# Gate stage of a PEER block: more first product in the steps with row products, upper halves at a step's begin, the high digit's one-hots for 32 tokens

## The chip, the cores and the metric

The kernel runs on one core of a Trainium2 chip. The metric is device microseconds of one execution. The kernel before took 1411.17 us (median of three runs, 1410.4 to 1411.97). Engine names are those of the profile: PE is the matrix engine (PEld its weight loads), DVE the vector engine, ACT the scalar engine, POOL the GpSimd engine, SP the engine that issues most loads.

## The reference

For 512 tokens of width 1024: a normalised input goes through a gating group and an attention group, their joined output is added to the input, and a PEER layer follows, with 16384 experts:

```python
q = (xb @ w_query)                               # 8 heads, 2 halves
sc = einsum('thpd,hpkd->thpk', q, sub_keys)      # 128 keys a half
s_top, i_top = top_k(sc, 16)                     # 16 x 16 candidates
best, pos = top_k(cand, 16)                      # 16 experts a head
g = softmax(best)
h = gelu(einsum('thkd,td->thk', expert_u[eidx], xb))
out = einsum('thk,thkd->td', g * h, expert_v[eidx])
```

So each token uses 128 of the 16384 experts, each with its own gate `g`.

## The kernel before

Of the 512 tokens, 128 gather their experts' rows at the end. The other 384 (three tiles of 128) are computed densely, and 64 of these are mixed: their expert inputs are gathered rows, too. The experts stand as 128 rows of 128. Per row b of experts:

- the **first product** of 320 tokens with the 128 experts of b is a matrix product over 8 slices of the width; each is split in an upper and a lower half, so that a slice costs three matmuls (`mm3`, lines 196 to 198, 128x320). One b is a "tile" of first product: 8 slices, 24 matmuls, then a Gelu on ACT (line 724).
- the tile's weights come by a 512 KB load (`raw`, line 155, SP's queue, three buffers); ACT makes the upper half (`hi`, line 157) and DVE or POOL the lower half (`lo`, line 158: raw minus hi). `hi` and `lo` have five buffers each.
- in the last and longest stage (from 600 us on) the gated activations are multiplied with the rows of V (line 1215), together with the first products that are left.

The **gate stage** lies ahead of that. It turns the 128 chosen experts of each of the 384 tokens into a dense table of gates in DRAM. It runs in 48 steps of 8 tokens (`TC`), and a block of matmuls follows two steps later (`LEAD`). Block m is the product of step m's tokens. A step n does:

- POOL: `bm` (line 981), the second one-hot with the gate in it, from two digit tables `hb` (high digit times gate, 8 wide) and `lb` (low digit, 16 wide).
- PE: block n-2, eight f32 matmuls `pa<-bm,am` (line 998; each stands as two in the profile).
- ACT: two copies `gst<-pa` (line 1001) of that block; after every second step it issues a 1024 KB store of `gst` (line 1005, three buffers).
- DVE: `am` (line 989), the first one-hot; three buffers of `am` and of `bm`.
- in steps 1 to 33 also a gathered row of U for the mixed tokens (POOL issues the gather, line 660) and its **row product** on DVE (`rowe`, line 670).
- every second step, the digits for the next 16 tokens on DVE (lines 970 and 973: `hb`, `hb` times gate, `lb`).
- `some` slices of first product on PE, and at the step's end sometimes one new tile: its load, its `hi` on ACT, its `lo` on DVE or (each fourth) on POOL.

Where a token tile ends, its gates are transposed on PE (lines 959 and 960). At step 33 the row products are through, and `dots` and `weights_early` fold them into the gates.

Order: PE, DVE, ACT and POOL take their instructions of this stage exactly as the code writes them (`manual_schedule`); each queue runs in order, and a waiting instruction holds all behind it. SP's loads are in the order of their issue and wait for a free `raw` buffer. The numbers of the table are `AHEAD` 25, `LAST` 2 and `HELD` 2; `steps` is 48, `own` is 40.

Of the kernel before, what the change touches and what calls it, by code (L numbers as in the profile page):

```python
# [8 lines left out]
F32 = mybir.dt.float32  # L9
F32R = mybir.dt.float32r  # L10
# [3 lines left out]
AF = mybir.ActivationFunctionType  # L14
ALU = mybir.AluOpType
# [4 lines left out]
P = 128  # L20
# [3 lines left out]
KT = D // P  # L24
# [27 lines left out]
BC = 2  # L52
# [3 lines left out]
RAW = 3  # L56
HI = 5
LO = 5
# [5 lines left out]
LEAD = 2  # L64
BH = 8
BL = NB // BH
QT = 16
AHEAD = 25
LAST = 2
HELD = 2  # L70
EASY = 8
SOME = 15
FILL = (0, 1, 2, 3, 4, 4, 3, 3)
# [21 lines left out]
def hybrid_block(tc, x, ln1, w_in, gng, wsT, bsb, qkg, bias, w_out, ln2, wq, skT, uT, ud, vd, out):  # L95
    nc = tc.nc
    ctx = ExitStack()
    with ctx:
# [13 lines left out]
        def big(tag, dt, bufs):  # L112
            return wst.tile([P, 1024], dt, name=tag, tag=tag, bufs=bufs)
# [10 lines left out]
        loads, splits, ready = [], [], []  # L124
# [24 lines left out]
        def load_split(src, eng=nc.vector, **dims):  # L149

            raw = big("raw", F32, RAW)
            hi = big("hi", F32R, HI)
            lo = big("lo", F32R, LO)
            fold = (lambda v: v.rearrange("p (a b) -> p a b", **dims)) if dims else (lambda v: v)
            load = nc.sync.dma_start(fold(raw), src)
            loads[:] = [getattr(load, "ins", load)]
            top = nc.scalar.activation(hi, raw, AF.Copy)  # L157
            ins = eng.tensor_tensor(lo, raw, hi.bitcast(F32), op=ALU.subtract)  # L158
            halved[:] = [getattr(i, "ins", i) for i in (top, ins)]
            if eng is nc.gpsimd:  # L160
                splits[:] = [getattr(ins, "ins", ins)]
            return fold(hi), fold(lo)

        def split_tile(i, eng):

            ready.append((*divmod(i, BC), load_split(uT[i], eng, b=P)))
# [257 lines left out]
        with tc.tile_pool(name="preb", bufs=1, reuse_waits="tile") as preb:  # L424
# [135 lines left out]
            steps = [(t, (h, h + 1)) for t in range(TT) for h in range(0, HB, 2)]  # L560
# [158 lines left out]
        def multiply_tile(whole=False):  # L719
            multiply_some(KT, whole)  # L720
# [215 lines left out]
        def split_next(eng=nc.gpsimd):  # L936
            nonlocal split
            if split < AHEAD * BC:
                split_tile(split, eng)
                split += 1  # L940

        for _ in range(HELD):
            split_next()
# [9 lines left out]
        gp = gp_ctx.enter_context(tc.tile_pool(name="gp", bufs=1, reuse_waits="tile"))  # L953

        def gates_of(t, ff):

            ps = pa()
            for i in range(3):
                nc.tensor.transpose(ps[:, i * P:(i + 1) * P], ff[:, i, :], ident)
            nc.tensor.transpose(ps[:, 3 * P:4 * P], gate[:, t, :], ident)  # L960
            return ps.rearrange("p (a t) -> p a t", a=4)

        def digits(g, q):

            ts_ = slice(q * QT, (q + 1) * QT)
            hb = gp.tile([P, QT, BH], F32, name="hb", tag="hb", bufs=2)
            lb = gp.tile([P, QT, BL], F32, name="lb", tag="lb", bufs=2)
            for i, (d, n) in enumerate(((hb, BH), (lb, BL))):
                full = [P, QT, n]
                nc.vector.tensor_tensor(d, iota_k[:, None, 0:n].to_broadcast(full),  # L970
                                        g[:, 1 + i, ts_, None].to_broadcast(full), op=ALU.is_equal)
                if i == 0:
                    nc.vector.tensor_tensor(d, d, g[:, 3, ts_, None].to_broadcast(full), op=ALU.mult)
            return hb, lb

        def second_one_hot(d, c):

            ts_ = slice(c * TC % QT, c * TC % QT + TC)
            full = [P, TC, BH, BL]
            bm = gp.tile([P, TC, P], F32, name="bm", tag="bm", bufs=LEAD + 1)  # L980
            nc.gpsimd.tensor_tensor(bm.rearrange("p t (h l) -> p t h l", l=BL),  # L981
                                    d[0][:, ts_, :, None].to_broadcast(full),
                                    d[1][:, ts_, None, :].to_broadcast(full), op=ALU.mult)
            return bm
# [9 lines left out]
        def products(am, bm, c, st):  # L994
            for q in range(TC // 4):
                ps = pa()
                for i in range(4):
                    nc.tensor.matmul(ps[:, i * P:(i + 1) * P], am[:, 4 * q + i, :], bm[:, 4 * q + i, :],  # L998
                                     start=True, stop=True)
                t0 = (c * TC + 4 * q) % TG  # L1000
                nc.scalar.copy(st[:, :, t0:t0 + 4], ps.rearrange("p (t b) -> p b t", b=NB))

        def store(n, st):
            gd, (n0, n1) = next((g, r) for g, r in zip(gds, GROUPS) if n < r[1])
            nc.scalar.dma_start(gd[:, :, n - n0, :].rearrange("q p f -> p q f"),
                                st.rearrange("p (q b) t -> p q (b t)", b=GB))
# [15 lines left out]
        steps = NDT // TC  # L1022
# [5 lines left out]
        own = steps - UX // TC  # L1028
        with tc.manual_schedule(engines=engines):
            multiply_tile()  # L1030
            gs[0] = gates_of(GT, ff.pop(0))
            dgs = {0: digits(gs[0], 0)}
            split_next()
            multiply_tile()
            for n in range(steps + LEAD):
                t, c = divmod(n, per)
                if n < steps:
                    bms[n] = second_one_hot(dgs[n * TC // QT], c)
                if n >= LEAD:
                    m = n - LEAD  # L1040
                    if m * TC % TG == 0:
                        st = gp.tile([P, NB, TG], F32, name="gst", tag="gst", bufs=3)
                    products(ams.pop(m), bms.pop(m), m % per, st)
                    if (m + 1) * TC % TG == 0:
                        store(m * TC // TG, st)
                while begun:
                    activate_tile()
                if n < steps:
                    ams[n] = first_one_hot(gs[t], c)
                if n in (1, 2):  # L1050
                    indices_early(NH - 3 + n)
                    ready_early(NH - 3 + n)
                if n:
                    dots_early(LAGE, 1)
                if EASY - 3 < n < own - 7 and n % 8 != 1:
                    gather_early(1, gat, ROWA)
                if t + 1 < ND:
                    if c == per - 5:
                        ff[t + 1] = indices_of(GT + t + 1)
                    if c == per - 3:  # L1060
                        gs[t + 1] = gates_of(GT + t + 1, ff[t + 1])
                if n == own - 7:
                    assert not early
                    dots_early(0)
                    weights_early(0)
                if n == own - 6:
                    weights_early(1)
                if n == own - 4:
                    weights_early(2)
                if n == own - 3:  # L1070

                    late = gates_of(GT + t, ff.pop(t))
                if n == own - 1:
                    gs[t] = late

                    gat_ctx.close()
                    gcp = [ctx.enter_context(tc.tile_pool(name="gcp", bufs=1, side="right", reuse_waits="tile"))]
                if n == steps - 2:
                    load_gates(0, nc.gpsimd, range(1))
                if (n + 2) * TC % QT == 0 and n + 2 < steps:  # L1080
                    t1, c1 = divmod(n + 2, per)
                    dgs[(n + 2) * TC // QT] = digits(late if n + 2 >= own else gs[t1], c1 * TC // QT)

                made = len(ready) * KT + (KT - open_tile[4] if open_tile else 0)
                left = (AHEAD - LAST) * BC * KT - split * KT + made
                some = -(-left // (steps + LEAD - n))
                multiply_some(some)
                if n > 1 and split < (AHEAD - LAST) * BC + HELD and len(ready) < HELD and (n > EASY or n % 2 == 0):
                    split_next(nc.vector if split % 4 else nc.gpsimd)
            while ready or open_tile:  # L1090
                if split == AHEAD * BC and not weights:
                    weights[0] = rows_of_v(0)
                multiply_tile()
                split_next(nc.vector)
                if len(begun) > 1:
                    activate_tile()
            while begun:
                activate_tile()
# [202 lines left out]
```

## Time and profile before

| what | value |
|---|---|
| median of three runs | 1411.17 us |
| profiled execution, own time | 1410.74 us |
| its span | 1409.0 us |
| around the span | 1.7 us |
| gate stage, blocks 0 to 10 | 438.6 to 473.4 us |
| blocks 11 to 33 (with row products) | 473.4 to 545.9 us |
| blocks 34 to 47 (without) | 545.9 to 584.5 us |
| last stage | from 600 us to the end |

All times of the trace are microseconds from the span's start. A window row gives, for each engine, its busy time and in brackets the instructions in that window, then PE's granted clock, the share of the DMA engines' time, and GB/s. In the chain of waits a row is: start, length, what. In a timeline row the bracket at the end is the idle time of that engine ahead of the instruction, and what ended it. Where a timeline merges rows, "x2" is their number. Groups of instructions give busy time and mean ns of one, then the idle time ahead of them. A busy PE is not a PE at its peak, since the ends of matmuls are modelled; so the distance between the starts of blocks says more than busy time.

### The profile page before, as it was taken

How to read it: one execution, taken by the hardware profiler on the slowest of the kernel's cores; microseconds unless marked ns; L12 is line 12 of the kernel's file. 1: busy time of each engine (PE TensorE's matmuls, PEld its weight loads, DVE VectorE, ACT ScalarE, POOL GpSimd, SP SyncE). 2: the span in 40 equal slices, each digit the busy share in tenths (PEclk: the TensorE clock that was granted, in tenths of full speed). 3: DMA queues.
4: the chain of work that ended last, by engine and by line, in shares of the span. 5: the costliest groups of instructions: out<-in, count | busy, mean ns of one | idle time of the engine just before them, and what ended most of it. 6: DMA issues, size and time to landing. Idle time of an engine off the chain costs nothing.

```text
span 1409.0 us, 21692 instructions
## 1 busy us (share of the span) xinstructions
PE 1386.7 (98%) x7838; PEld 1224.6 (87%) x7838; DVE 1154.3 (82%) x2508; ACT 612.0 (43%) x960; POOL 673.0 (48%) x486
## 2 busy tenths in 40 slices
PE   9999999999999989999999999999999999999998
PEld 7887688899899989988898899899889989888887
DVE  5437845898998998678999999898898887889983
ACT  5447635443434445534344444444443333333331
POOL 0002103777778998424555456454464543344520
PEclk9999999999999999999999999999999999999999
DMA  4452316567666999979999999999999998799981
GB/s 165 135 194 76 104 72 199 193 220 271 240 225 222 348 354 281 289 254 355 330 342 348 362 360 342 369 372 359 375 348 383 352 359 337 272 353 363 357 311 60
DMA packets 164330, 396.24 MB, mean 281 GB/s; under 512 B 12880, under 2 KB 75232, under 8 KB 162176
## 3 DMA queue, kind: packets, MB, share of 16 engines
q1 hardware_dynamic: 64640, 194.14, 37.6%
q0 software_dynamic: 48176, 173.46, 33.9%
q10 hardware_dynamic: 51408, 27.27, 6.6%
q8 instruction: 61, 1.00, 0.3%
q14 instruction: 45, 0.37, 0.1%
HBM read 363.34 MB, written 31.46 MB: 280 GB/s over the span
## 4 chain that ended last, share of the span: by engine, by line
PE 78%; DVE 13%; DMA 2%; POOL 2%; issue 2%; ACT 2%; ACTq 0%; DVEq 0%; POOLq 0%
PE pa L1215 23%; PE px L1215 12%; PE pu L196 9%; PE pu L198 9%; PE pu L197 9%; PE pa L998 3%; PE pa L196 3%; PE pa L197 3%; PE pa L198 3%; DVE rowe L670 2%; DVE lo L158 2%; DVE tree L800 1%; DVE am L989 1%; DMA raw<-in_vd 1%; POOL rowe L660 1%
## 5 line engine op out<-in xcount | busy, mean ns | idle before, releaser
L157 ACT ACTIVATE hi<-raw 128x1024 fp32r<-128x1024 f32 x296 | 313.0, 1058 | 448.2 <-DMA raw<-in_uT 120.8
L158 DVE TENSOR_TENSOR lo<-raw,hi 128x1024 fp32r<-128x1024 f32 x244 | 305.7, 1254 | 99.9 <-ACT hi L157 99.1
L1139 POOL DMA_INDIRECT row<-in_ud,eint x128 | 193.0, 1508 | 180.8 <-DVE acc L1152 129.4
L196 PE MATMUL pu<-xch,hi 128*128 128x320 f32 x784 | 247.5, 316 | 3.0 <-ACT act L724 2.8
L1150 POOL DMA_INDIRECT row<-in_vd,eint x128 | 159.7, 1247 | 178.0 <-DVE row L1141 118.6
L198 PE MATMUL pu<-xch,lo 128*128 128x320 f32 x784 | 242.8, 310 | 0.8 <-DVE lo L158 0.8
L197 PE MATMUL pu<-xcl,hi 128*128 128x320 f32 x784 | 242.8, 310 | 0.0
L1215 PE MATMUL pa<-lo,wh 128*128 128x512 f32 x512 | 199.7, 390 | 0.0
L1215 PE MATMUL pa<-hi,wh 128*128 128x512 f32 x512 | 199.4, 389 | 0.0
L158 POOL TENSOR_TENSOR lo<-raw,hi 128x1024 fp32r<-128x1024 f32 x52 | 124.0, 2398 | 119.0 <-ACT hi L157 116.1
L1152 DVE SCALAR_TENSOR_TENSOR acc<-row,hw,acc 128x1024 f32<-128x1024 f32 x128 | 165.2, 1290 | 2.8 <-DMA row<-in_vd,eint 2.5
L1141 DVE SCALAR_TENSOR_TENSOR row<-row,xb 128x1024 f32<-128x1024 f32 x128 | 155.7, 1220 | 10.3 <-DMA row<-in_ud,eint 10.3
L1215 PE MATMUL pa<-hi,wl 128*128 128x512 f32 x512 | 158.5, 389 | 0.0
L196 PEld LDWEIGHTS pu<-xch,hi 128*128 128x128 f32 x784 | 148.0, 189 | 6.1 <-ACT act L724 4.4
L197 PEld LDWEIGHTS pu<-xcl,hi 128*128 128x128 f32 x784 | 148.1, 189 | 1.4
L198 PEld LDWEIGHTS pu<-xch,lo 128*128 128x128 f32 x784 | 147.8, 189 | 1.1 <-DVE lo L158 1.0
L1215 PEld LDWEIGHTS pa<-hi,wh 128*128 128x128 f32 x512 | 96.1, 188 | 20.5
L1215 PEld LDWEIGHTS pa<-hi,wl 128*128 128x128 f32 x512 | 96.1, 188 | 20.3
L1215 PEld LDWEIGHTS pa<-lo,wh 128*128 128x128 f32 x512 | 96.1, 188 | 20.2
L998 PE MATMUL pa<-bm,am 128*128 128x128 f32 x768 | 95.1, 277 | 8.0 <-POOL bm L981 4.2
L998 PEld LDWEIGHTS pa<-bm,am 128*128 128x128 f32 x768 | 90.7, 191 | 11.7 <-POOL bm L981 6.5
L1215 PE MATMUL px<-hi,wh 128*128 128x512 f32 x256 | 100.1, 391 | 0.4 <-ACT hi L157 0.4
(236 smaller groups left out, 2641.6 us busy)
## 6 DMA issues: line engine op xcount, KB each, us to landing
raw<-in_uT SPq DMA_DIRECT2D x128, 512.0 KB
raw<-in_vd SPq DMA_DIRECT2D x128, 512.0 KB
gd<-gst ACTq DMA_DIRECT2D x24, 1024.0 KB
gc<-gd SPq DMA_DIRECT2D x15, 1280.0 KB
raw<-in_w_in SPq DMA_DIRECT2D x19, 512.0 KB
raw<-in_wq SPq DMA_DIRECT2D x16, 512.0 KB
raw<-in_w_out SPq DMA_DIRECT2D x8, 512.0 KB
gc<-gd SPq DMA_DIRECT2D x15, 256.0 KB
```

The costliest lines, as they stand in the source:

```text
L157: top = nc.scalar.activation(hi, raw, AF.Copy)
L158: ins = eng.tensor_tensor(lo, raw, hi.bitcast(F32), op=ALU.subtract)
L196: nc.tensor.matmul(ps, lh[0], rh[0], start=first, stop=False)
L197: nc.tensor.matmul(ps, lh[0], rh[1], start=False, stop=False)
L198: nc.tensor.matmul(ps, lh[1], rh[0], start=False, stop=last)
L670: nc.vector.scalar_tensor_tensor(row, row, 1.0, xbu, op0=ALU.mult, op1=ALU.mult, accum_out=du[:, j:j + 1])
L998: nc.tensor.matmul(ps[:, i * P:(i + 1) * P], am[:, 4 * q + i, :], bm[:, 4 * q + i, :], start=True, stop=True)
L1139: nc.gpsimd.indirect_dma_start(out=row, out_offset=None, in_=ud, in_offset=bass.IndirectOffsetOnAxis(ap=eint[:, j:j + 1], axis=0))
L1141: nc.vector.scalar_tensor_tensor(row, row, 1.0, xb0, op0=ALU.mult, op1=ALU.mult, accum_out=hw[:, j:j + 1])
L1150: nc.gpsimd.indirect_dma_start(out=row, out_offset=None, in_=vd, in_offset=bass.IndirectOffsetOnAxis(ap=eint[:, j:j + 1], axis=0))
L1152: nc.vector.scalar_tensor_tensor(acc0, row, hw[:, j:j + 1], acc0, op0=ALU.mult, op1=ALU.add)
L1215: nc.tensor.matmul(accs[t][half], (wh, wh, wl)[k][:, b, tok], w[b][k % 2][:, ds_], start=first and k == 0, stop=last and k == 2)
```

## The change

Three edits, all in the gate stage:

1. The number of slices of first product in a step, `some`. Before, what is left is spread evenly over the steps that are left. Now a step ahead of step 35 (`own - 5`) counts three times (`LATE`) as much as one of the last 15.
2. A new tile's load and its upper half on ACT are issued at the step's begin (`split_begun`), ahead of the block's copies; only the lower half stays at the step's end (`finish`). The condition lets one more tile wait in line (`len(ready) <= HELD` in place of `<`).
3. The high digit's one-hots are made for 32 tokens at a time, every fourth step, in place of 16 every second step. The low digit's stay at 16.

```diff
+LATE = 3
+        def split_begun(i):
+            raw, hi, lo = big("raw", F32, RAW), big("hi", F32R, HI), big("lo", F32R, LO)
+            load = nc.sync.dma_start(raw.rearrange(...), uT[i].rearrange(...))
+            loads[:] = [getattr(load, "ins", load)]
+            nc.scalar.activation(hi, raw, AF.Copy)
+            def finish(eng):
+                eng.tensor_tensor(lo, raw, hi.bitcast(F32), op=ALU.subtract)
+                ready.append((*divmod(i, BC), [v.rearrange(...) for v in (hi, lo)]))
+            return finish
...
         def digits(g, q):
-            ts_ = slice(q * QT, (q + 1) * QT)
-            hb = gp.tile([P, QT, BH], F32, name="hb", tag="hb", bufs=2)
-            lb = gp.tile([P, QT, BL], F32, name="lb", tag="lb", bufs=2)
...
+            w = 2 * QT
+            if q % 2 == 0:
+                ts_ = slice(q * QT, q * QT + w)
+                hb = one_hot("hb", 0, BH, ts_)
+                nc.vector.tensor_tensor(hb, hb, g[:, 3, ts_, None].to_broadcast([P, w, BH]), op=ALU.mult)
+                high[:] = [hb]
+            return high[0][:, q % 2 * QT:(q % 2 + 1) * QT], one_hot("lb", 1, BL, slice(q * QT, (q + 1) * QT))
...
             for n in range(steps + LEAD):
                 t, c = divmod(n, per)
+                halved_now = []
+                if n > 1 and split < (AHEAD - LAST) * BC + HELD and len(ready) <= HELD and (n > EASY or n % 2 == 0):
+                    halved_now = [(split_begun(split), nc.vector if split % 4 else nc.gpsimd)]
+                    split += 1
...
-                left = (AHEAD - LAST) * BC * KT - split * KT + made
-                some = -(-left // (steps + LEAD - n))
+                left = (AHEAD - LAST) * BC * KT - split * KT + made + len(halved_now) * KT
+                some = -(-left * LATE // (LATE * max(0, own - 5 - n) + min(steps + LEAD - n, steps + LEAD - own + 5)))
                 multiply_some(some)
-                if n > 1 and split < (AHEAD - LAST) * BC + HELD and len(ready) < HELD and (n > EASY or n % 2 == 0):
-                    split_next(nc.vector if split % 4 else nc.gpsimd)
+                for finish, eng in halved_now:
+                    finish(eng)
```

What this does to PE's order is seen first at the end of the stage. Rows of PE from block 42 on, before (lines 196 to 198 are one slice of first product; the tiles are those named above):

```order
L998 MATMUL pa<-bm,am 128x128 x8
L196 MATMUL pu<-xch,hi 128x320
L197 MATMUL pu<-xcl,hi 128x320
L198 MATMUL pu<-xch,lo 128x320
L196 MATMUL pu<-xch,hi 128x320
L197 MATMUL pu<-xcl,hi 128x320
L198 MATMUL pu<-xch,lo 128x320
L998 MATMUL pa<-bm,am 128x128 x8
```

Two slices, six matmuls, stand behind each of the blocks 11 to 46. And PE's rows of the same place now, from block 38 on (the line numbers are those of the changed kernel, 13 to 24 higher):

```order
L1018 MATMUL pa<-bm,am 128x128 x8
L209 MATMUL pu<-xch,hi 128x320
L210 MATMUL pu<-xcl,hi 128x320
L211 MATMUL pu<-xch,lo 128x320
L1018 MATMUL pa<-bm,am 128x128 x8
L209 MATMUL pu<-xch,hi 128x320
L210 MATMUL pu<-xcl,hi 128x320
L211 MATMUL pu<-xch,lo 128x320
L1018 MATMUL pa<-bm,am 128x128 x64
```

The blocks 36 to 39 are followed by one slice each, and the blocks 40 to 47 by none (64 matmuls in a row). The blocks 11 to 30 are now followed by three slices, 31 to 35 by two as before, and 1 to 10 by three as before.

On DVE, the rows around the last row products, before (steps 33 to 36):

```order
L989 TENSOR_TENSOR am<-iota_k,pa 128x1024
L670 SCALAR_TENSOR_TENSOR rowe,du<-rowe,px 128x1024 x3
L686 COPY dots<-du 64x8x8
L989 TENSOR_TENSOR am<-iota_k,pa 128x1024
L970 TENSOR_TENSOR hb<-iota_k,pa 128x128
L973 TENSOR_TENSOR hb<-hb,pa 128x128
L970 TENSOR_TENSOR lb<-iota_k,pa 128x256
L989 TENSOR_TENSOR am<-iota_k,pa 128x1024 x2
```

and now:

```order
L1009 TENSOR_TENSOR am<-iota_k,pa 128x1024
L683 SCALAR_TENSOR_TENSOR rowe,du<-rowe,px 128x1024 x3
L699 COPY dots<-du 64x8x8
L173 TENSOR_TENSOR lo<-raw,hi 128x1024
L1009 TENSOR_TENSOR am<-iota_k,pa 128x1024
L985 TENSOR_TENSOR hb<-iota_k,pa 128x256
L992 TENSOR_TENSOR hb<-hb,pa 128x256
L985 TENSOR_TENSOR lb<-iota_k,pa 128x256
L1009 TENSOR_TENSOR am<-iota_k,pa 128x1024 x2
```

A lower half now stands at the end of step 33, ahead of the `am` of step 34, and the high digit's two instructions are twice as wide. Over the stage DVE's lower halves stood at the ends of steps 2, 4, 6, 9, 11, 14, 22, 26, 30, 38, 42 and 46, and POOL's at 8, 18 and 34; now DVE's stand at 2, 4, 6, 9, 10, 12, 17, 20, 22, 28, 30 and 33, and POOL's at 8, 14 and 25. So 15 tiles are split in the stage before and now.

ACT's order at the stage's begin shows the second edit (block m's copies belong to step m+2). Before, steps 2 and 3:

```order
L724 ACTIVATE act<-pu 128x320 x4
L1001 COPY gst<-pa 128x128x4 x2
L157 ACTIVATE hi<-raw 128x1024
L1001 COPY gst<-pa 128x128x4 x2
L1005 DMA gd_4555<-gst 128x16x128
```

and now:

```order
L737 ACTIVATE act<-pu 128x320 x4
L170 ACTIVATE hi<-raw 128x1024
L1021 COPY gst<-pa 128x128x4 x4
L1025 DMA gd_4555<-gst 128x16x128
L737 ACTIVATE act<-pu 128x320
L170 ACTIVATE hi<-raw 128x1024
```

The upper half of step 2's tile stood behind the copies of block 0 and stands ahead of them now. So it is for each of the 15 tiles: its place on ACT moves up by the two copies of one block.

More of the change, by code (lines that the diff above doesn't have):

```diff
@@ L162, in load_split @@
             return fold(hi), fold(lo)
+        def split_begun(i):
+            raw, hi, lo = big("raw", F32, RAW), big("hi", F32R, HI), big("lo", F32R, LO)
+            load = nc.sync.dma_start(raw.rearrange("p (a b) -> p a b", b=P), uT[i].rearrange("p (a b) -> p a b", b=P))
+            loads[:] = [getattr(load, "ins", load)]
+            nc.scalar.activation(hi, raw, AF.Copy)
+            def finish(eng):
+                eng.tensor_tensor(lo, raw, hi.bitcast(F32), op=ALU.subtract)
+                ready.append((*divmod(i, BC), [v.rearrange("p (a b) -> p a b", b=P) for v in (hi, lo)]))
+            return finish
         def split_tile(i, eng):
@@ L961, in gates_of, with one_hot @@
             return ps.rearrange("p (a t) -> p a t", a=4)
+        high = []
         def digits(g, q):
-            ts_ = slice(q * QT, (q + 1) * QT)
-            hb = gp.tile([P, QT, BH], F32, name="hb", tag="hb", bufs=2)
-            lb = gp.tile([P, QT, BL], F32, name="lb", tag="lb", bufs=2)
-            for i, (d, n) in enumerate(((hb, BH), (lb, BL))):
-                full = [P, QT, n]
+            w = 2 * QT
+            def one_hot(name, i, n, ts_):
+                full = [P, ts_.stop - ts_.start, n]
+                d = gp.tile(full, F32, name=name, tag=name, bufs=2)
                 nc.vector.tensor_tensor(d, iota_k[:, None, 0:n].to_broadcast(full),
                                         g[:, 1 + i, ts_, None].to_broadcast(full), op=ALU.is_equal)
-                if i == 0:
-                    nc.vector.tensor_tensor(d, d, g[:, 3, ts_, None].to_broadcast(full), op=ALU.mult)
-            return hb, lb
+                return d
+            if q % 2 == 0:
[4 more added lines that the diff above has]
+            return high[0][:, q % 2 * QT:(q % 2 + 1) * QT], one_hot("lb", 1, BL, slice(q * QT, (q + 1) * QT))
         def second_one_hot(d, c):
```

## The prediction

> **What bounds the kernel now.** I read the page's first part and its chain, then windows by stage, then the chain of waits within the gate stage.
>
> ```profile
> PE 1386.7 (98%) x7838; PEld 1224.6 (87%) x7838; DVE 1154.3 (82%) x2508; ACT 612.0 (43%) x960; POOL 673.0 (48%) x486
> PE 78%; DVE 13%; DMA 2%; POOL 2%; issue 2%; ACT 2%; ACTq 0%; DVEq 0%; POOLq 0%
> ```
>
> PE bounds the program: 98% busy, 78% of the chain. The change leaves PE's work as it is; it only moves it. So it can win only time in which PE waits, and the question is where that is. By stage (blocks 0 to 10, 11 to 33, 34 to 47, then the last stage):
>
> ```profile
> 438.60:473.40 34.80, 34.02 (x274) 33.75 (x273) 29.77 (x43) 19.95 (x32) 30.34 (x19) 1.00 0.82 251
> 473.40:545.90 72.50, 65.68 (x516) 62.25 (x514) 71.52 (x114) 33.98 (x58) 67.45 (x43) 1.00 1.06 351
> 545.90:584.50 38.60, 37.41 (x308) 37.18 (x309) 24.05 (x35) 19.77 (x34) 28.27 (x15) 1.00 0.86 248
> 600.00:1409.00 809.00, 802.23 (x4188) 709.33 (x4186) 701.68 (x1188) 317.71 (x457) 365.13 (x264) 1.00 0.89 333
> ```
>
> In blocks 11 to 33 DVE is busy 71.5 of 72.5 us and POOL 67.5, while PE has its gap. In blocks 34 to 47 DVE has 24 of 38.6, POOL 28: there PE sets the pace. In the last stage PE is short of full by under 7 us of 809, so what the gate stage ends earlier by, the end is earlier by. What PE needs for a block is seen in the chain of waits, where it follows PE alone:
>
> ```profile
> 451.83 1.78 PE pa L998 x16
> 454.94 1.78 PE pa L998 x16
> ...
> 544.59 1.23 DVE am L989
> 545.96 2.04 PE pa L998 x16
> 548.00 1.95 POOL bm L981
> 549.99 2.05 PE pa L998 x16
> 552.04 0.33 PE pa L959 x3
> ...
> 561.36 1.78 PE pa L998 x16
> 564.03 1.78 PE pa L998 x16
> ...
> 582.70 1.80 PE pa L998 x16
> ```
>
> A block is 1.78 us. With nine matmuls of first product behind it (early rows) the next starts after 3.11, with six (late rows) after 2.67; so a slice of three costs 0.44 to 0.45. One slice would be 2.22, none 1.78. Blocks 11 to 33 need 23 x 2.67 plus two sets of gate transposes at about 0.5 (0.33 for three of the four, row above, and an estimate of 0.15 for the last): 62.4 us. They took 72.5: PE loses **10 us** there, since `am` and `bm` come late. Block 34 at 545.96 follows the `am` that ends at 545.8, behind the last row products.
>
> **The late blocks.** From block 34's start to block 47's: 582.70 - 545.96 = 36.7 us. Now 34 and 35 keep two slices (5.3, plus 0.5 for a transpose), 36 to 39 have one (8.9), 40 to 46 none (12.5): 27.2 us, **9.5 less**. In it is 1.5 us of waiting at block 35, whose `bm` stood on POOL behind a lower half that now stands at step 25. Does something else bind at 1.78? POOL:
>
> ```profile
> L981 POOL TENSOR_TENSOR bm<-hb,lb 128x1024 f32<-128x1024 f32 x26 | 50.5, 1951 | 0.3
> L158 POOL TENSOR_TENSOR lo<-raw,hi 128x1024 fp32r<-128x1024 f32 x2 | 4.8, 2381 | 0.9 <-ACT hi L157 0.7 <-issue 0.2
> ```
>
> At 1.9 a `bm` it loses 0.1 us a block over the last eight, and it has gained more than that over blocks 36 to 39 (2.22 each): covered. A 1024 KB store each 3.56 us is 295 GB/s, under the 351 of the middle window: covered, but close.
>
> **The middle blocks.** PE: 20 blocks with three slices, 3 with two: 62.2 + 8.0 + 1.0 = 71.2 us, under 72.5. So PE itself still fits; 8.9 us of work goes into its gap. But the tiles must be split sooner, and that is DVE's work, which has no gap:
>
> ```profile
> L989 DVE TENSOR_TENSOR am<-iota_k,pa 128x1024 f32<-128x1024 f32 x24 | 29.1, 1212 | 0.0
> L158 DVE TENSOR_TENSOR lo<-raw,hi 128x1024 fp32r<-128x1024 f32 x6 | 12.4, 2065 | 1.2 <-ACT hi L157 1.2
> ...
> L158 DVE TENSOR_TENSOR lo<-raw,hi 128x1024 fp32r<-128x1024 f32 x5 | 6.3, 1250 | 10.0 <-ACT hi L157 10.0
> ```
>
> The upper two rows are the stretch from the lower half of step 9 to the end of step 33, the lowest is the time after it. Ahead of step 34's `am`, from step 9's end on, DVE has nine lower halves now (9, 10, 12, 17, 20, 22, 28, 30, 33), six before (9, 11, 14, 22, 26, 30). Three more at 2065 ns, less the 0.08 by which instructions overlap: **+6.0 us**. One took 1.21 to 3.25 here, and 1.25 in the late window, so three cost 3.4 to 9.5; I take the mean of the place that they move to.
>
> [...]
>
> The digits give some back:
>
> ```profile
> 478.11 0.28 DVE L970 TENSOR_TENSOR hb<-iota_k,pa 128x128 f32<-128x128 f32 x1
> 478.42 0.29 DVE L973 TENSOR_TENSOR hb<-hb,pa 128x128 f32<-128x128 f32 x1
> 478.63 0.41 DVE L970 TENSOR_TENSOR lb<-iota_k,pa 128x256 f32<-128x256 f32 x1
> 478.96 1.21 DVE L989 TENSOR_TENSOR am<-iota_k,pa 128x1024 f32<-128x1024 f32 x1
> ```
>
> One set is 0.31 + 0.21 + 0.33 = 0.85, two are 1.70. A 128x256 `hb` isn't in the trace; by the `lb` row of that size it takes 0.44 with its dependent follower, and the product 0.33: 0.44 + 0.33 + 2 x 0.33 = 1.43. Six pairs: **-1.6** (between 0 and -3). The upper halves' earlier place takes waits from DVE:
>
> ```profile
> 455.55 1.28 DVE L158 TENSOR_TENSOR lo<-raw,hi 128x1024 fp32r<-128x1024 f32 x1 [1.95 <-ACT hi L157]
> 465.73 3.01 DVE L158 TENSOR_TENSOR lo<-raw,hi 128x1024 fp32r<-128x1024 f32 x1 [1.24 <-ACT hi L157]
> ```
>
> An upper half now runs a whole block (3.11) sooner, so both vanish. The second counts in full, of the first perhaps 1 us, since DVE can't run more than three `am` ahead of PE: **-2.2** (0 to -3.2). The waits of 10 us in the late window cost nothing before, with PE busy. POOL gets one more lower half (2.4 us) ahead of step 34, at whose end it stood idle for 1.9 until DVE's `dots` came:
>
> ```profile
> 544.88 0.77 POOL L688 DMA_DIRECT2D dots<-du  x1 [1.88 <-DVE dots L686]
> L157 ACT ACTIVATE hi<-raw 128x1024 fp32r<-128x1024 f32 x18 | 19.0, 1058 | 1.6 <-issue 1.6
> ```
>
> Its `bm` for step 34 was through at 543.0 and would be at 545.4, before an `am` that itself comes some 2 us later: nothing, as long as DVE is the later one (0.5 us or more if it isn't). On ACT an upper half of 1.06 us (second row) now delays the copies behind it by as much. That hides behind the 3.11 us that PE has until the next block: a copy is needed only when PE comes round to its PSUM bank, half a block or more later. Where gates hold a bank it may show, up to 1 us a time; that is in the next term. Last, PE had 2.67-us blocks to catch up with after a stall, and now needs 3.11 of some 3.2: 0.7 us for stalls not caught up (estimate: of the 10 us, the part that short blocks no longer win back; 0 to 3). Middle: 6.0 - 1.6 - 2.2 + 0.7 = **+2.9** (bounds -2 to +9).
>
> **The way into the last stage.** It starts from the gates' load:
>
> ```profile
> 575.82 0.61 POOL L1015 DMA_DIRECT2D gc<-gd  x1
> 585.27 0.90 DVE L1181 TENSOR_TENSOR act<-act,gc 128x320 f32<-128x320 f32 x2 [4.49 <-DMA gc<-gd]
> 595.34 0.51 PE L1215 MATMUL px<-hi,wh 128*128 128x512 f32 x1 [0.37 <-ACT hi L157]
> ```
>
> The load is issued behind `bm` of step 46 and lands 9.4 us later; DVE waits 4.5 for it, and PE, with first products between, only 0.4. With blocks of 1.78, that issue is some 3 us nearer to the last block's end, so DVE's queue (with the next lower half, whose buffer the second row of V needs) starts later against PE. PE has 55 matmuls there instead of 50, 0.7 us more cover. I take **+1.0** (0 to 5).
>
> **Sum** against the profiled execution's 1410.74: -9.5 + 2.9 + 1.0 = -5.6, 1405.1. The median shown is 0.4 above that execution: **1405.5 us**. What would be the most: the middle at -2, the way in at 0 gives 1399.7.
>
> **Rivals.**
>
> *Transfers set the middle's pace.* Three loads of 0.52 MB move into a window that moves 351 GB/s at a share of 1.06:
>
> ```profile
> 500.00:515.00 15.00, 13.52 (x105) 12.47 (x104) 14.87 (x24) 6.79 (x12) 14.27 (x10) 1.00 1.09 371
> SPq L155 <- DVE lo L158: 120.1, 16, 13.3
> ACT gst L1001 <- DMA gd<-gst: 4.2, 2, 3.0
> ```
>
> 72.5 us x 351 is 25.4 MB, with the three 27.0. At 351 that is 76.9 us, +4.4 in place of +2.9: 1407.0. Against it: 371 in one window, and loads that wait for a buffer (120 us) rather than for the wire. For it: stores that already kept ACT waiting twice.
>
> [...]
>
> *The way in eats the gain.* If the gates' load is held up by the stores, now one per 3.56 us, the 4.5 us of the row above grow by those 3 and PE has no cover left: +4 more, 1409.5.
>
> *Slower: upper halves hold up ACT.* An upper half now stands ahead of a block's copies. If its load hasn't landed, the copies wait behind it, the PSUM banks stay full, and PE stops for the whole lateness. A load's buffer is free when the lower half three tiles earlier is through; for the tiles of steps 10 and 12 that is only four steps earlier, and the upper half's turn comes two steps before DVE's:
>
> ```profile
> 589.00 5.21 DMA raw<-in_vd
> ```
>
> Two steps are 6.2 us, against 5.2 for such a load in a crowded moment. If the crowded middle doubles that to 10.4, each of these two tiles stops PE by 4.2, and each of the eight after them, with two to three steps more, by perhaps 1: +16 and 1421 at its full price; it decides from a sum of 6 us on, i.e. from loads of 8.5 us. Against it: no row of before has ACT waiting for `raw<-in_uT` in the stage.
>
> *The change does less than it says* holds in part: PE's order has three slices instead of two in twenty blocks, none anywhere three times as much. The sums above count by that order.
>
> **Chances.** Forecast 0.58 (its own range 1401.5 to 1408.5), transfers 0.15, lock 0.08, way in 0.09, slower 0.10. A measurement of this kernel tells 0.2%, 2.8 us, from no change: faster below 1408.3. Faster: 0.55 of the forecast, 0.11 of transfers, 0.04 of the rest: 0.70. Same: 0.03 + 0.04 + 0.11 = 0.18. Slower: 0.12 (the last rival, and 0.02 from the others). The range: 1401 to 1411.5, from a free middle to the way in and the lock together; it leaves out the slower case.
>
> **What would show it.** Right: blocks 40 to 47 start 1.78 to 1.95 us apart; block 34 starts about 3 us after 545.96 and block 47 near 576; DVE over 95% busy in blocks 11 to 33, its lower halves there near 2 us; no wait of DVE for `hi` there; PE's wait ahead of `px` under 2 us. Wrong: late blocks at 2.2 or more with ACT waiting for `gd<-gst`; ACT waiting for `raw<-in_uT` ahead of `hi`; the middle over 78 us; or a first matmul of the last stage that waits 4 us or more for `gc`.

## The result, and the profile after

The change takes **1403.28 us** (median of four runs, 1400.82 to 1404.62), the kernel before 1411.57 (median of four, 1410.4 to 1412.97). The ratio is 0.9934, with a 95% interval of 0.9921 to 0.9947: faster by 0.5 to 0.8%. The profiled execution took 1400.82 us, the lowest of the four.

The changed kernel's page (first part), and its windows by stage, for blocks 0 to 10, 11 to 33, and from 34 to just past block 47's start:

```profile
span 1398.7 us, 21680 instructions
PE 1384.0 (99%) x7838; PEld 1224.0 (88%) x7838; DVE 1154.9 (83%) x2484; ACT 613.9 (44%) x960; POOL 671.5 (48%) x486
436.70:472.50 35.80, 33.98 (x274) 33.72 (x272) 33.55 (x44) 20.14 (x32) 33.73 (x22) 1.00 0.89 276
472.50:545.70 73.20, 72.88 (x574) 72.64 (x574) 72.36 (x100) 37.80 (x62) 69.06 (x42) 0.98 1.06 354
545.70:575.90 30.20, 29.70 (x253) 29.37 (x254) 19.96 (x26) 16.75 (x30) 24.10 (x14) 1.00 0.88 250
```

PE has as many matmuls as before (7838) and less time without one. In blocks 11 to 33 it does 574 in 73.2 us, where it did 516 in 72.5. What that takes from the late blocks is seen in PE's own order. Rows of the changed kernel's timeline, PE alone:

```profile
472.59 3.18 PE L1018 MATMUL pa<-bm,am 128*128 128x128 f32 x16 [1.91 <-DVE ff L902]
...
545.78 2.02 PE L1018 MATMUL pa<-bm,am 128*128 128x128 f32 x16 [0.31 <-DVE am L1009]
...
560.78 9.98 PE L1018 MATMUL pa<-bm,am 128*128 128x128 f32 x88
571.19 4.73 PE L1018 MATMUL pa<-bm,am 128*128 128x128 f32 x40 [0.42 <-DVE am L1009]
...
588.24 0.50 PE L1239 MATMUL px<-hi,wh 128*128 128x512 f32 x1 [0.93 <-ACT hi L158]
```

The row at 560.78 is 88 matmul instructions without anything between: five and a half blocks, 1.8 us each. From block start to block start, in the profiled executions of all kernels of this study (in us; the last column runs to the end of the span):

| kernel | block 0 at | 0 to 11 | 11 to 34 | 34 to 47 | from 47 on |
|---|---|---|---|---|---|
| before | 438.6 | 34.8 | 72.6 | 36.6 | 826.4 |
| **the change** | 436.8 | 35.8 | 73.2 | **28.2** | 824.8 |
| e1_late_only | 437.5 | 34.9 | 83.2 | 30.5 | 827.0 |
| e2_begun_only | 439.3 | 35.8 | 72.7 | 36.9 | 829.5 |
| e3_digits_only | 438.3 | 35.1 | 72.8 | 36.3 | 827.9 |
| e4_no_digits | 438.2 | 35.8 | 73.7 | 28.2 | 826.3 |
| e5_hi_at_end | 436.7 | 36.1 | 76.1 | 28.2 | 826.1 |
| e6_not_after_bm_pair | 437.2 | 33.7 | 74.4 | 35.0 | 828.8 |
| e7_not_before_ff | 435.9 | 33.7 | 74.4 | 34.7 | 825.1 |
| e8_late2 | 437.7 | 35.8 | 76.1 | 35.3 | 825.3 |
| e9_gap_in_e6 | 437.7 | 33.7 | 74.8 | 34.4 | 827.8 |
| e10_gap_in_after | 438.5 | 35.9 | 73.3 | 28.2 | 825.1 |
| e11_keep_33 | 436.7 | 33.7 | 74.8 | 28.2 | 825.3 |
| e12_gates_load_sp | 438.0 | 33.7 | 74.7 | 28.2 | 826.6 |

The two profiled spans differ by 10.3 us: 1.8 ahead of block 0, -1.0 up to block 11, -0.6 up to 34, 8.4 up to 47, 1.7 behind. The first and the last of these are no part of the change that can be told: block 0, ahead of which the code is nearly the same, starts anywhere from 435.9 to 439.3, and the stretch from block 47 took 824.8 to 829.5 in these fourteen executions. The gate stage itself gave 6.7.

What the change did on DVE is best seen over blocks 0 to 33 as a whole. Groups of DVE instructions by line, first of the kernel before from 438.6 to 545.9 (with its window row), then of the change from 436.7 to 545.7:

```profile
L158 DVE TENSOR_TENSOR lo<-raw,hi 128x1024 fp32r<-128x1024 f32 x9 | 17.2, 1914 | 4.8 <-ACT hi L157 4.8
L970 DVE TENSOR_TENSOR hb<-iota_k,pa 128x128 f32<-128x128 f32 x17 | 4.7, 279 | 0.3 <-POOL bm L981 0.3
L973 DVE TENSOR_TENSOR hb<-hb,pa 128x128 f32<-128x128 f32 x16 | 4.6, 287 | 0.6
438.60:545.90 107.30, 99.69 (x788) 96.00 (x786) 101.29 (x156) 53.93 (x90) 97.79 (x61) 1.00 0.98 318
```

```profile
L1009 DVE TENSOR_TENSOR am<-iota_k,pa 128x1024 f32<-128x1024 f32 x33 | 40.0, 1211 | 2.0 <-PE pa L1018 2.0
L173 DVE TENSOR_TENSOR lo<-raw,hi 128x1024 fp32r<-128x1024 f32 x12 | 24.3, 2026 | 0.0
L985 DVE TENSOR_TENSOR hb<-iota_k,pa 128x256 f32<-128x256 f32 x9 | 3.7, 409 | 0.0
L992 DVE TENSOR_TENSOR hb<-hb,pa 128x256 f32<-128x256 f32 x8 | 3.4, 421 | 0.3
436.70:545.70 109.00, 106.86 (x848) 106.36 (x846) 105.91 (x143) 57.94 (x94) 102.78 (x63) 0.98 1.00 328
```

Three more lower halves cost 7.1 us of DVE (17.2 to 24.3); the high digits' tables gave back 2.2 (4.7 + 4.6 to 3.7 + 3.4); the 4.8 us of waiting for `hi` are gone. DVE is busy 4.6 longer and idle 2.9 shorter (6.0 to 3.1), so these 34 blocks take 1.7 longer. At 105.9 of 109.0 it has hardly a gap left.

### The profile page after: what moved, and what is told of

Read it like the earlier page. It is cut to its first block, busy times and chain, and to the rows that moved or that the text cites. A ratio compares the mean times of both kernels' runs of the same rounds, so it can differ in the third digit from the quotient of the medians.

```text
span 1398.7 us, 21680 instructions
## 1 busy us (share of the span) xinstructions
PE 1384.0 (99%) x7838; PEld 1224.0 (88%) x7838; DVE 1154.9 (83%) x2484; ACT 613.9 (44%) x960; POOL 671.5 (48%) x486
## 4 chain that ended last, share of the span: by engine, by line
PE 43%; DVE 7%; DMA 4%; issue 2%; ACT 0%; POOL 0%; DVEq 0%; ACTq 0%; POOLq 0%
PE pa L1239 20%; PE px L1239 10%; PE pu L209 4%; PE pu L211 4%; PE pu L210 4%; DVE lo L159 2%; DMA row<-in_ud,eint 2%; DVE row L1165 2%; DMA row<-in_vd,eint 1%; DVE acc L1176 1%; DMA raw<-in_vd 0%; DVE act L1205 0%; DVE wl L1207 0%; DVE rep L755 0%; DVE tree L813 0%
## 5 line engine op out<-in xcount | busy, mean ns | idle before, releaser
L158 ACT ACTIVATE hi<-raw 128x1024 fp32r<-128x1024 f32 x281 | 297.1, 1058 | 457.5 <-DMA raw<-in_uT 136.1
L159 DVE TENSOR_TENSOR lo<-raw,hi 128x1024 fp32r<-128x1024 f32 x232 | 284.7, 1228 | 85.0 <-ACT hi L158 84.7
L159 POOL TENSOR_TENSOR lo<-raw,hi 128x1024 fp32r<-128x1024 f32 x49 | 117.0, 2403 | 116.9 <-ACT hi L158 113.2
L1239 PE MATMUL px<-lo,wh 128*128 128x512 f32 x256 | 100.3, 392 | 0.0
```

The lines of the kernel that those rows point to most:

```text
L1239: nc.tensor.matmul(accs[t][half], (wh, wh, wl)[k][:, b, tok], w[b][k % 2][:, ds_], start=first and k == 0, stop=last and k == 2)
```

## The experiments

Twelve kernels were run beside the kernel before; all of them compute the whole reference. Ratios are to the kernel before. "Edit 1" is the formula with `LATE`, "edit 2" the upper halves at the step's begin, "edit 3" the digits for 32 tokens.

### One part alone, and the change without one part

**e1: edit 1 alone**, in the kernel before:

```
+LATE = 3
-some = -(-left // (steps + LEAD - n))
+some = -(-left * LATE // (LATE * max(0, own - 5 - n) + min(steps + LEAD - n, steps + LEAD - own + 5)))
```

> Edit 1 alone: the kernel before with the new count of first product per step (three slices behind blocks 11 to 30, none behind 40 to 47), upper halves at a step's end and 16-token digits as before. Theory (PE's work is fixed, the late blocks give about 9 us, and edits 2 and 3 only keep the crowded middle from taking it back): faster than before by 4 to 6 us, with blocks 34 to 47 in 28 us and blocks 11 to 33 in 75 to 77 us, DVE waiting for upper halves again. Rival (edits 2 and 3 are worth nothing): faster by 8 us, like the whole change.

Measured: ratio 0.998 (0.9967 to 0.9992). The late blocks got 6 us shorter, the middle 10.7 longer, more than either side had allowed. This holds for the profiled execution, which is the slowest of e1's twelve (1415.03 us, their median is 1410.10), so the usual loss is smaller. Its window of blocks 11 to 33, its lower halves there, and its waits from 472 to 556 (sum, times, longest):

```profile
472.40:555.70 83.30, 74.63 (x577) 72.73 (x575) 80.72 (x116) 37.70 (x62) 71.19 (x44) 0.98 1.02 329
L159 DVE TENSOR_TENSOR lo<-raw,hi 128x1024 fp32r<-128x1024 f32 x7 | 18.9, 2699 | 1.9 <-ACT hi L158 1.9
PE pa L999 <- DVE am L990: 7.8, 6, 2.4
POOL dots L689 <- DVE dots L687: 6.2, 1, 6.2
POOL lo L159 <- ACT hi L158: 2.9, 1, 2.9
```

Seven lower halves took 18.9 us where the same number takes 13.5 in the change: 5.4 us more. Which of the two other edits saves that was the next question.

**e2: edit 2 alone** (the change with `LATE = 1` and the old `digits`), and **e3: edit 3 alone** (the kernel before with the new `digits`):

> Edit 2 alone: upper halves at a step's begin and one more tile in line, first product spread as before, 16-token digits. Theory: the late blocks stay at 2.67 us each; only DVE's waits for upper halves in blocks 2 to 10 go, so faster by 0 to 2 us. Rival (the gain came from the upper halves, since they free DVE): faster by 4 us or more, with the middle blocks shorter than 70 us.

> Edit 3 alone: the high digit's one-hots for 32 tokens in the kernel before. Theory: DVE has 1.6 us less to do ahead of block 34, so faster by 0.5 to 1.6 us, no verdict at the noise of this kernel. Rival (DVE isn't the bound of the middle, POOL's second one-hots are): 0.

Measured: 1.0001 (0.9989 to 1.0014) and 1.0002 (0.9992 to 1.0012). Neither does anything by itself that can be told: with PE's slices where they were, the late blocks stay at 36 to 37 us and the middle at 72.7.

**e4: edits 1 and 2, without 3** (the change with the old `digits`):

> The whole change without edit 3. Theory: slower than the change by 0.5 to 1.6 us, so faster than before by 6.5 to 8. Rival (the middle is now bound by PE at 3.11 us a block, and DVE's work no longer counts): equal to the change within 0.3 us.

Measured: 0.9938 (0.9921 to 0.9954), against 0.9934 for the change. The middle is 73.7 in place of 73.2. So the digits are worth some 0.5 us in the profiles and nothing that the times can tell. Edits 1 and 2 make the gain: alone 0.2% and nothing, together 0.62%.

**e5: the change, with the upper halves alone back at the step's end** (orders of PE, DVE and POOL as in the change):

```
 def split_begun(i):
-    nc.scalar.activation(hi, raw, AF.Copy)
     def finish(eng):
+        nc.scalar.activation(hi, raw, AF.Copy)
         eng.tensor_tensor(lo, raw, hi.bitcast(F32), op=ALU.subtract)
```

> The whole change, with the upper halves alone put back: same steps for the tiles, same orders of PE, DVE and POOL, but on ACT each upper half stands behind its block's copies again. Theory formed from edit 1 alone (its middle took 83.2 us instead of 73.2, since an upper half behind copies that wait for PE makes DVE's lower half late, DVE's am late, and PE late again): middle blocks 80 us or more, total faster than before by 2 to 4 us only. Rival (edit 1 alone lost its time because its lower halves stood at other steps, 19, 24, 32, next to POOL's back-to-back one-hots): middle 74 us or less, faster than before by 7 to 8.5 us.

Measured: 0.9963 (0.9949 to 0.9977), about 4 us over the change by ratio; the middle is 76.1. My theory wanted 80 or more, since I took `hi`'s place on ACT for what had cost e1 its 10 us; that fell, and so did the rival's 74 or less. `hi`'s place is worth 3 us in the profiles and about 4 by the ratios. Edit 2 does more than that: it issues the load sooner, and it picks the step of a new tile by another condition, which puts the **lower halves** at other steps. In e1 those at steps 19, 24, 32 and 36 took 3.5 to 5.4 us. In the profiles this rest is the larger part of e1's loss (83.2 to 76.1), but e1's is its slowest execution; by the ratios, e1 at 0.998 to e5 at 0.9963, it is some 2 us. No run isolates it.

### What a lower half costs, by where it stands

The change's own lower halves are uneven too. DVE's, then POOL's rows of its timeline at the ends of steps 9 and 33:

```profile
459.25 5.21 DVE L173 TENSOR_TENSOR lo<-raw,hi 128x1024 fp32r<-128x1024 f32 x1
...
543.28 1.23 DVE L173 TENSOR_TENSOR lo<-raw,hi 128x1024 fp32r<-128x1024 f32 x1
```

```profile
457.19 2.41 POOL L173 TENSOR_TENSOR lo<-raw,hi 128x1024 fp32r<-128x1024 f32 x1
459.53 3.84 POOL L1001 TENSOR_TENSOR bm<-hb,lb 128x1024 f32<-128x1024 f32 x2
...
543.56 0.77 POOL L701 DMA_DIRECT2D dots<-du  x1 [0.91 <-DVE dots L699]
```

The one at 459.25 waits through the end of POOL's own lower half and through two `bm` (to 463.37) and ends 1.09 after. The one at 543.28 meets POOL waiting for `dots` and takes 1.23. So I moved them away from such places.

**e6: no new tile at steps 9, 17, 25 and 33; e7: nor at step 10.**

```
-if n > 1 and ... and (n > EASY or n % 2 == 0):
+if n > 1 and ... and (n > EASY or n % 2 == 0) and n % 8 != 1:                (e6)
+if n > 1 and ... and (n > EASY or n % 2 == 0) and n % 8 != 1 and n != 10:    (e7)
```

> The change, with no tile begun in the steps 9, 17, 25 and 33, in which POOL has no gather and makes two bm in a row: the tiles move to the next step. Theory (a lower half on DVE that starts next to two bm in a row waits for both: 5.21 us at step 9, 3.68 at step 17): DVE's lower halves of the middle fall to 1.2 to 2.2 us each, and the change gets 1 to 3 us faster. Rival (PE at 3.11 us a block is the bound of the middle now, DVE's time there is hidden): within 0.5 us of the change.

> As the run before, and no tile begun in step 10 either, so that no lower half stands between am of step 10 and the index work of step 11, whose PSUM bank PE waits for. Theory: the 5.2 us between the starts of blocks 10 and 11 fall back to 3.1 to 3.5 us, and of blocks 11 and 12 to 3.6 to 4.2: 2 to 3.5 us faster than the change in all. Rival (the wait comes from elsewhere, or blocks 12 and on run into the lower halves that moved there): within 1 us of the change.

Measured: 0.9977 (0.9968 to 0.9986) and 0.9957 (0.9944 to 0.9971), both worse than the change. Blocks 0 to 10 became 2.1 us shorter, as meant; but 1.2 of it comes back in the middle, and the late blocks grew from 28.2 to 35. The new condition shuts step 33, too, and so it put the last lower half at step 34. e6's timeline there, DVE, POOL and PE:

```profile
545.61 5.63 DVE L173 TENSOR_TENSOR lo<-raw,hi 128x1024 fp32r<-128x1024 f32 x1
```

```profile
544.42 5.72 POOL L1001 TENSOR_TENSOR bm<-hb,lb 128x1024 f32<-128x1024 f32 x3
```

```profile
545.26 1.95 PE L1018 MATMUL pa<-bm,am 128*128 128x128 f32 x16
552.51 3.75 PE L1018 MATMUL pa<-bm,am 128*128 128x128 f32 x16 [4.42 <-DVE am L1009]
556.06 0.85 PE L972 MATMUL pa<-ident,ff 128*128 128x128 f32 x3
```

With no gather left to issue, POOL makes three `bm` in a row, up to 550.14. The lower half, come at 545.61, ends at 551.24, 1.10 after the last of them. The `am` behind it is late, PE stands 4.42 us, and its next block takes 3.75 instead of 1.95. e6's windows of these blocks show why (the number behind the five engines is PE's granted clock):

```profile
545.20:547.90 2.70, 2.70 (x24) 2.62 (x22) 2.70 (x3) 1.24 (x3) 2.70 (x2) 1.00 0.68 195
552.50:555.50 3.00, 2.98 (x14) 3.00 (x15) 2.84 (x4) 0.58 (x1) 0.00 (x0) 0.50 0.43 156
555.50:558.00 2.50, 2.50 (x15) 2.50 (x15) 1.66 (x3) 0.59 (x1) 1.65 (x1) 0.66 0.04 11
558.00:561.00 3.00, 3.00 (x28) 3.00 (x26) 1.72 (x3) 1.17 (x2) 1.25 (x2) 1.00 1.00 291
```

After the wait the clock is granted at 0.50, then at 0.66 on the mean of the next window, and it is full in the last. So of the 6.8 us by which these blocks exceed the change's, 4.4 are the wait and the clock has about 2 more in it (3.75 less 1.95, and slower transposes).

**e8: `LATE = 2`**, which keeps two slices behind blocks 26 to 37 and one behind 38 to 42 (the expectation has 39 and 44):

> The change with a weight of 2 in place of 3: blocks 26 to 39 keep two slices, 40 to 44 one, 45 to 47 none. PE's work in blocks 34 to 47 is 31.1 us instead of 27.2. Theory: the middle is paced by PE at 3.11, so it gets shorter by 5 x 0.44 = 2.2 us and the late blocks longer by 3.1 to 3.9: slower than the change by 1 to 2 us. Rival (the weight hardly matters once the late blocks are under POOL's 1.9 us a one-hot): within 0.5 us of the change.

Measured: 0.9997 (0.9988 to 1.0007): the whole gain is gone. Fewer slices go early, so the last lower halves stand at steps 31 and 35, beside POOL's runs of three. e8's timeline, DVE, then POOL:

```profile
535.93 6.03 DVE L173 TENSOR_TENSOR lo<-raw,hi 128x1024 fp32r<-128x1024 f32 x1
551.62 4.50 DVE L173 TENSOR_TENSOR lo<-raw,hi 128x1024 fp32r<-128x1024 f32 x1
```

```profile
535.16 5.71 POOL L1001 TENSOR_TENSOR bm<-hb,lb 128x1024 f32<-128x1024 f32 x3
549.30 5.72 POOL L1001 TENSOR_TENSOR bm<-hb,lb 128x1024 f32<-128x1024 f32 x3
```

They end at 541.96 and 556.12, 1.09 and 1.10 after POOL's runs; PE waited 3.15 and 3.34 for what stood behind them. Of the 7.1 us by which e8's late blocks exceed the change's, 2.2 are the five slices more that they hold; the middle holds five fewer and is yet 2.9 longer.

**e9 and e10: something between the `bm`.** If the lower half only needs a moment in which POOL does something else, a tiny instruction behind each `bm` should let it in. e9 is e6, e10 the change, each with

```
+gap = gp.tile([P, 1], F32, name="gap", tag="gap", bufs=1)
 ...                                   # behind each bm:
+nc.gpsimd.memset(gap, 0.0)
```

> The kernel of e6 (whose lower half at step 34 took 5.63 us on DVE, while POOL made three bm in a row) with one more instruction on POOL: a one-column memset behind each bm, which reads nothing from SBUF. Theory (a lower half on DVE waits for the end of POOL's whole run of tensor_tensor, and gets in as soon as anything else stands between them): no lower half of DVE over 3.2 us, the one at step 34 at 1.2 to 3.2, blocks 34 to 47 in 28 to 31 us instead of 35, faster than e6 by 2 to 5 us. [...]

> The change with the same one-column memset on POOL behind each bm. Theory: DVE's lower halves at steps 9 and 17 (5.21 and 3.68 us) fall to 3.2 or less, the stall of PE at blocks 11 and 12 shrinks by 1 to 2 us; POOL has some 0.1 us more per step, which is hidden at 3.11 us a block: faster than the change by 0 to 2 us. Rival (POOL is itself as tight as PE in the middle: 67 of 72.5 us before): slower than the change by 1 to 3 us.

Measured: 0.9973 (0.9963 to 0.9984) for e9, e6's time; 0.9954 (0.9938 to 0.9969) for e10, no gain over the change. e9's timeline, POOL, then DVE:

```profile
545.28 1.96 POOL L1002 TENSOR_TENSOR bm<-hb,lb 128x1024 f32<-128x1024 f32 x1
547.16 0.13 POOL L1005 MEMSET gap<- 128x1 f32 x1
547.21 1.96 POOL L1002 TENSOR_TENSOR bm<-hb,lb 128x1024 f32<-128x1024 f32 x1
549.08 0.12 POOL L1005 MEMSET gap<- 128x1 f32 x1
549.13 1.94 POOL L1002 TENSOR_TENSOR bm<-hb,lb 128x1024 f32<-128x1024 f32 x1
```

```profile
546.47 5.69 DVE L173 TENSOR_TENSOR lo<-raw,hi 128x1024 fp32r<-128x1024 f32 x1
```

The lower half still ends at 552.16, 1.09 after the third `bm`, and in e10 the one at step 9 still takes 5.32. A memset of one column is no opening.

**e11: no new tile at steps 9 and 17 only**, which keeps the last one at step 33:

```
+if n > 1 and ... and (n > EASY or n % 2 == 0) and n not in (9, 17):
```

> The change with no tile begun in steps 9 and 17 alone, so that the last lower half stays at step 33, where POOL waits for the row products' result. Lower halves on DVE at 10, 11, 12, 18, 20, 22, 28, 30, 33. Theory (what undid e6 is the lower half that slipped from step 33 to step 34, beside POOL's run of bm): blocks 34 to 47 in 28 us as in the change, blocks 0 to 33 as in e6 or shorter (109.0 us in the change, 108.1 in e6): faster than the change by 0.5 to 2 us and than e6 by 6 to 8. Rival (tiles at other steps spoil the middle): no faster than e6.

Measured: 0.9927 (0.9912 to 0.9942). e11's lower halves on DVE stand where e6's do, but for the last, which is at step 33 instead of 34 (and POOL's last, at 25 instead of 26). Its row on DVE, and POOL's at that time:

```profile
542.75 1.22 DVE L173 TENSOR_TENSOR lo<-raw,hi 128x1024 fp32r<-128x1024 f32 x1
```

```profile
543.04 0.77 POOL L701 DMA_DIRECT2D dots<-du  x1 [0.74 <-DVE dots L699]
```

That one takes 1.22 instead of 5.63, and the late blocks 28.2 instead of 35.0: e11 is 0.5% faster than e6. This is the cleanest of the comparisons: between the two kernels only one tile on DVE and one on POOL stand a step apart, and it is the one on DVE that comes right ahead of the late blocks. Against the change it isn't told apart; the 2.1 us that it wins up to block 11 come back as 1.6 in the middle, where DVE is again the one without a gap (busy 73.57 of 74.80 us).

### The way into the last stage

**e12: e11, with the gates' first load issued by SP two steps sooner:**

```
-if n == steps - 2: load_gates(0, nc.gpsimd, range(1))
+if n == steps - 4: load_gates(0, nc.sync, range(1))
```

> The kernel of e11 with the gates' first load (1280 KB, on the way into the last stage) issued by SP two steps sooner in the code, instead of POOL behind the bm of step 46. In the change it was issued at 570.34 and landed at 579.5, 3.7 us behind the last block's end; DVE waited 8.4 us for it and PE 0.9. Theory (the way in hangs on this load, and what it can still win is PE's 0.9 to 1.3 us): the load lands 2 to 6 us sooner, PE's wait ahead of the first px goes to 0 to 0.4, faster than e11 by 0.5 to 1.5 us, hardly to be told from no change. Rival (the load waits for the stores of the gates ahead of it, or takes from the late stores what it gains): same landing, or ACT waiting for stores in blocks 44 to 47, no faster or slower by up to 2 us.

Measured: 0.9939 (0.9925 to 0.9952): nothing gained. The change's rows of this place, then e12's:

```profile
570.40 0.60 POOL L1035 DMA_DIRECT2D gc<-gd  x1
579.51 0.89 DVE L1205 TENSOR_TENSOR act<-act,gc 128x320 f32<-128x320 f32 x2 [8.38 <-DMA gc<-gd]
```

```profile
576.79 0.90 DVE L1205 TENSOR_TENSOR act<-act,gc 128x320 f32<-128x320 f32 x2 [5.00 <-DMA gc<-gd]
580.73 2.36 DVE L159 TENSOR_TENSOR lo<-raw,hi 128x1024 fp32r<-128x1024 f32 x2 [3.05 <-ACT hi L158]
```

DVE's wait for `gc` fell from 8.4 to 5.0, and 3.05 for `hi` came in behind it. PE's wait ahead of `px` was 0.92 us, as in the change (0.93); in e11, from which e12 differs by this load alone, it was 1.30 and DVE's wait 8.43. So the earlier load won PE about 0.4 us, which the times can't tell.

## Why the prediction was right, and where its sizes were off

The forecast was 1405.5 us, 5.6 less than before, and 1403.28 was measured, 8.3 less by the medians: the sign and the range held, the gain was larger. The profiles trace 6.7 of it to the gate stage, of which the way in took 0.6 back; what goes beyond that lies ahead of block 0 and in the last stage, and no step of the prediction made it. By its steps:

- **The late blocks: forecast 27.2 us (9.5 less), measured 28.2 (8.4 less).** Right in mechanism. Blocks 40 to 47 start 1.8 apart but for 2.5 once, no store and no `bm` on POOL sets a slower pace there. The missing 1 us is 0.7 at that one place, in block 45 (the 0.42 us at 571.19 are part of it), and 0.3 in blocks 36 to 39, at 2.2 to 2.5 instead of 2.2.
- **The middle: forecast 2.9 longer, measured 1.7 over blocks 0 to 33** (1.0 up to block 11, 0.6 behind). This is the term of the sum that was mis-sized most. Inside it, errors of both signs: the three lower halves took 7.1 (forecast 6.0), the digits gave back 2.2 (1.6), the waits for `hi` gave all of their 4.8 (2.2), of which 2.0 turned into waits of `am` for PE, where DVE had run as far ahead as its buffers let it. The reason for each stands, and DVE has no gap left (72.36 busy of 73.20 us). But in this execution PE sets the pace there: from block 12 to block 31 its blocks start 3.11 apart, with one exception of 3.55 at a gate transpose. What the middle has over the 71.2 us that the prediction gave PE is nearly all PE at half clock behind block 11 (half of 3.41 us, 1.7; see the last section), which the prediction didn't have. That the term came out near the forecast is partly luck.
- **PE has one new wait** that no step of the prediction named: 1.91 us ahead of block 11, behind the index work `ff` of the gate transposes, which the 5.21-us lower half at step 9 had made late. e6, e7, e11 and e12, without that lower half, are 2.1 us shorter up to there.
- **The way in: forecast +1.0, measured +0.6** (a PE wait of 0.93 in place of 0.37). DVE's wait for `gc` nearly doubled, from 4.49 to 8.38, since the load still lands 9.1 us after its issue and all that it waits with came sooner; the first products covered it, as said.
- **Digits alone** were costed at -1.6 on the path; e3 and e4 give 0 to 0.5. DVE's time fell as computed, but what DVE saves there is partly waited for elsewhere.

Of the rivals, **transfers** fell: 354 GB/s in the middle, and its waits list none of ACT for `gd<-gst`. **Slower, with ACT held up** fell: ACT had no wait for `raw<-in_uT` up to block 34. **The way in** cost PE 0.6 more, far from the 5 of that rival. The **lock** of the chances, on which the range's upper end counts too, is a highest price for a lower half on DVE beside POOL's `bm`. It was closest to deciding, and no run shows that price: 3.68 and 5.21 us were measured in the change, 5.63 in e6 and 6.03 in e8. The rows here show a wait for up to three of POOL's instructions (e6's ends 1.10 us after the last of three `bm`, those of e8 1.09 and 1.10).

So the forecast held for a reason that it didn't contain. The late gain of 8.4 needs the last lower half to stand at step 33, where POOL waits for `dots`. One step later (e6), or with steps 31 and 35 (e8, less the 2.2 us of its slices), 5 to 7 us of it are lost. The prediction summed the late blocks on PE's needs and on POOL's mean `bm` of 1.95, and had no term for a lower half among them, since none stands there in the change. That the last one falls at step 33 was no choice of the prediction's: in that part it was luck.

The parts do not add up singly: 0.998, 1.0001 and 1.0002 alone, 0.9934 together. Edit 1 brings the late gain and pays for it in the middle, where lower halves meet POOL's runs and `hi` comes late; edit 2 takes most of that back and has nothing to win without edit 1. Its size beside edit 1 is 9.5 us of the middle by the profiles (83.2 to e4's 73.7), and some 6 us by the ratios (0.998 to 0.9938), which don't rest on e1's slowest execution. How this splits stays open: 3 to 4 us are `hi`'s place (e5), and the rest, for the places of the lower halves or the earlier load, was not measured by itself.

## What to carry to other kernels

Where an instruction waits for another engine's, as DVE's lower halves do here, its cost is set by what stands on that engine at that moment: read its rows one by one (the spread of 1.22 to 6.03 us, not the mean of 2.07), and place it where the other engine waits or issues a transfer (1.23 us at step 33 of the change, 1.22 in e11). A table or formula that moves work also moves where the last of such instructions falls, so look at that place before trusting a sum of means. And test edits in pairs: one that frees time on an engine can show nothing until another uses it (edit 2 alone 1.0001, edit 1 alone 0.998, the two together 0.9938).

## What the runs showed of the hardware that was not expected

**A lower half on DVE can wait for a whole run of POOL's instructions.** In the fourteen profiles 112 of the gate stage's 168 lower halves on DVE took over 1.3 us (1.22 when free). In all 112 the end stands 1.07 to 1.10 us after the end of one of POOL's `bm` or `lo`. In 18 cases POOL had a further such instruction right behind the running one, and DVE waited for that, too, up to the last of the run. But in seven cases it got in between two `bm`, as in this pair of the kernel with edit 2 alone (POOL, then DVE), where the two `bm` take 4.80 instead of 3.82:

```profile
548.65 4.80 POOL L994 TENSOR_TENSOR bm<-hb,lb 128x1024 f32<-128x1024 f32 x2 [2.34 <-DVE lb L983]
```

```profile
549.52 2.13 DVE L173 TENSOR_TENSOR lo<-raw,hi 128x1024 fp32r<-128x1024 f32 x1
```

What decides between the two stays open. Six of the seven lie in the first 11 blocks, right behind a wait of DVE for `hi` (1.1 to 1.6 us); this one doesn't, and one of e5's that came behind such a wait (0.78 us, at 491.21) waited for both. Why the memset lets no lower half in (5.69 us in e9, 5.32 in e10) is open as well; other instructions between (a larger one, or one that reads) weren't tried.

**A wait of PE can cost more than its length.** Behind a wait of 4.42 us (e6) the granted clock was 0.57 on the mean of the next 5.5 us, so 0.50 for some 4.7 of them by estimate; behind 4.08 (e7) it was 0.50 for the whole 3.6 us from 550.9 to 554.5. After 3.15 (e8, at 543.24) the next block took 2.02, as after a short wait; after 3.34 (e8) the clock was 0.71, then 0.59. Even the 1.91 of the change was followed by it: its block at 472.59 takes 3.18, at 0.68 and then 0.50:

```profile
472.50:474.50 2.00, 1.91 (x11) 1.94 (x12) 2.00 (x2) 0.40 (x1) 1.84 (x2) 0.68 1.01 402
474.50:476.50 2.00, 2.00 (x11) 2.00 (x11) 2.00 (x5) 0.78 (x2) 1.58 (x2) 0.50 1.08 392
476.50:479.00 2.50, 2.50 (x21) 2.50 (x21) 2.50 (x4) 1.13 (x2) 2.35 (x2) 0.97 0.86 279
```

In e4, e8 and e10 a like wait of 1.86 to 2.02 us was followed by a block of 2.02, and the clock was 1.00 from there to block 34 in e4 and e10. So nearly the same gap costs another 1 to 2 us in one execution and nothing in another. In the traces of the kernel before and of the change the record of the granted clock has 1 and 0.50 alone. It has 0.50 twice in each: for 3.41 us from 631.05 and from 473.22, and behind PE's last matmul (which ends at 1405.06 and 1394.83), from 1409.29 and from 1398.23. The two begin 778.24 and 925.01 us apart, 228.0 and 271.0 times 3.413. In the 3.41 us ahead of the first one PE was busy for 0.44 of the time in both (627.64 to 631.05, and 469.81 to 473.22, in which the change's wait lies whole). With these two traces cut into stretches of that length, to both sides of it, none of over 800 others is under 0.58 up to PE's last matmul, and the clock is 1 behind all of them. Whether the place of a wait among such stretches decides was not shown; no run varied it on purpose. The kernel before has its one drop ahead of the end in the last stage, at 631.05; the change has none there, which can be a part of the 1.7 us behind block 47.

So the change's 72.88 us of busy PE in the middle hold stretched matmuls (its block 11 takes 3.18 us, e10's 2.02). e10's middle, without the drop, takes as long (73.3) with PE busy 71.98 and DVE 72.70: there PE waits for DVE instead. Neither engine has much to spare in the middle now.
